# Staged tiles stored from ScalarE's queue, pair 0's splits three products earlier, down-stage loads in order of use

## The chip, the cores and the metric

The kernel runs on one core of one Trainium2 chip. The metric is the device time of one execution in microseconds (us); the time before is the median of three executions. TensorE multiplies; VectorE (DVE), ScalarE (ACT) and GpSimd (POOL) do the elementwise work; SyncE (SP) issues nearly all transfers between the chip's memory and SBUF. Every engine works through its own queue of instructions in order, and an instruction that has to wait holds what stands behind it in the same queue.

## What is computed

The reference is one layer of a flow model: a branch of state-space scans and a Fourier branch, gated and added to the residual, and then a gated feed-forward network with a final norm. The change lies in the feed-forward network:

```python
h2 = rmsnorm(x, p["norm2_g"]) * (1.0 + scale2) + shift2
ff = (jax.nn.silu(h2 @ p["w_ffn_gate"]) * (h2 @ p["w_ffn_up"])) @ p["w_ffn_down"]
x = x + gate2 * ff
```

There are 1152 tokens (1024 of the sample, 128 of the prompt), the model's width is 1024 and the hidden width 2816. All of it is in fp32.

## The kernel before, in words

**Up stage.** The hidden width is 22 tiles of 128, taken as 11 pairs, p = 0 to 10. For each pair `ffn_unit` (L1129 and on) runs a gate unit ("g") and an up unit ("u"). A unit multiplies a 2 x 2 arrangement of weight blocks by seven products, a Winograd scheme (Z W X Y Z X Y in the names of the PSUM banks), for two groups of tokens A and B. Each fp32 matmul is three matmuls in the fast fp32r form, on a high and a low part. So every weight operand is split: a cast on ScalarE (L962), then a subtraction on GpSimd or VectorE (L963). Sums of weight blocks (L1194 to L1210) are made on GpSimd. The unit's results are gated on ScalarE and GpSimd (L1188, L1190), stored to `ffd` in memory (L1229), and the sample's part of the pair is fetched again as `ra` (L1127) into the single buffer "gb".

**Operands for the down stage.** The down product is a Winograd scheme too, for pairs 0 to 8; pairs 9 and 10 use four ordinary products (STD). `a_steps(m)` makes pair m's seven operands out of `ra`, spread as hooks over the 14 products of the next pair's two units: for each a cast by ScalarE into a ring of three staging slots `stg` (L1307), the low part on VectorE (L1308), and a store to `ad` in memory (L1310). Pair 0 comes last, during pair 10's units. Three of its seven operands (ki 2, 3, 4) are not stored but stay in the staging ring. The list of hooks says after which product each step is issued; the first six products of the 14 have none:

```python
return [no, no, no, no, no, no, do(0), do(1), do(5), p6, do(p7a, 6), do(2), do(3), do(p7b, 4)]
```

**Down stage.** Block 0 is pair 0 alone; blocks 1 to 4 hold two pairs each (1 and 2, up to 7 and 8); then comes the STD block. `load_w` (L1394) fetches down weights `wd`, `prep` makes their Winograd sums (L1409) and splits them into `B` (L1362 and L1363; for pair 0 into `B0P`, with the subtraction on GpSimd), `load_at` (L1374) fetches operands `A` back from `ad`, `load_p` (L1405) the prompt's part `pr`, `load_a` (L1380) the raw tiles `fr` of pairs 9 and 10, and `x1_load` (L1535) the residual. The matmuls are on L1443, their sums into `acc` on L1460 and L1462. Pair 0's first two operands come as one tile `A1` in the buffer "gb", so their load waits for the last use of `ra0`.

**What sets the order.** The program is written as above, and a scheduler merges the pieces into one queue per engine by its own estimate of times. All loads and stores named here are in the SP queue. `tc.issue_after(x)` keeps an instruction behind x in the order. Tiles with the same tag share a ring of buffers, so a load waits until the last reader of the buffer's previous tile is done.

Of the kernel before, what the change touches and what calls it, by code (L numbers as in the profile page):

```python
# [19 lines left out]
NS = 1024  # L20
# [41 lines left out]
def tile_flow_step(ctx: ExitStack, tc: tile.TileContext, a, o):  # L62
    nc = tc.nc
    V, S, PL, PE, SY = nc.vector, nc.scalar, nc.gpsimd, nc.tensor, nc.sync
# [23 lines left out]
    def f32(ap):  # L88
        return ap.bitcast(F32)
# [38 lines left out]
    mods, last = {}, {}  # L128
# [179 lines left out]
    def load_w(q):  # L308
        wu[q] = weight(a["w_in"][q], f"us{q}", pool=pwu if q > 1 else None, eng=V)
# [24 lines left out]

    ada1_head()
    load_w(0)
    norm_stats(0)
    norm_tr(0)
    load_s5()
    load_w(1)  # L340
    h_scale0(range(4))
    u_first(0)
# [3 lines left out]
    norm_tr(1)  # L346
    run(ada1[5:])
    load_w(2)
    load_w(3)
    h_scale0(range(4, 8))  # L350
# [597 lines left out]
    x1d = dram.tile([9, 128, D], F32, tag="x1d", name="x1d")  # L948
# [150 lines left out]
    ffd = dram.tile([NF, 128, TOK], F32, tag="ffd", name="ffd")  # L1099
# [20 lines left out]
    LO, HI = slice(0, 512), slice(512, 1024)  # L1120
# [149 lines left out]
    hk, no = h2_hooks(2), (lambda: None)  # L1270
# [17 lines left out]
    ad = {m: dram.tile([7, 128, 2, 512], F32, tag=f"ad{m}", name=f"ad{m}") for m in range(STD[0])}  # L1288
# [3 lines left out]
    def a_steps(m):  # L1292
        a_ = {f"{f}{z}": ra[m][:, f, h] for f in range(2) for z, h in (("L", LO), ("H", HI))}

        def comb(out, x, y, op=ALU.subtract):
            V.tensor_tensor(a_[out], a_[x], a_[y], op)  # L1296

        def p6():
            comb("0H", "0H", "1H", ALU.add)
            comb("0L", "0H", "0L")  # L1300

        def one(ki):
            nonlocal nstg
            src = a_[dict(P1="0L", P2="1L", P6="0L", P7="0L", P4="1H", P5="0H", P3="1L")[KEYS[ki]]]
            st_ = stg[:, nstg % 3]
            nstg += 1
            S.copy(out=st_[:, 0], in_=src)  # L1307
            V.tensor_tensor(st_[:, 1], src, f32(st_[:, 0]), ALU.subtract)  # L1308
            if m or ki not in (2, 3, 4):
                SY.dma_start(out=ad[m][ki], in_=f32(st_))  # L1310

        def do(*fs):
            return lambda: [one(f) if isinstance(f, int) else f() for f in fs]

        p7a, p7b = (lambda: comb("1L", "1L", "0L")), (lambda: comb("0L", "1H", "0L"))
        return [no, no, no, no, no, no, do(0), do(1), do(5), p6, do(p7a, 6), do(2), do(3), do(p7b, 4)]

    for p in range(1, NF // 2):
        hk = a_steps((p - 1) % STD[0]) if p > 1 else [no] * 14
        ffn_unit(p, "g", "AB", hk[:7])  # L1320
        ffn_unit(p, "u", "AB", hk[7:])
        if p == 2:
            ffn_unit(0, "g", "B")
            ffn_unit(0, "u", "B")
            ra_load(2)
        if p == NF // 2 - 2:
            ra_load(0)
# [14 lines left out]
    AT, BT, PT, raws, araw, wraw = {}, {}, {}, {}, {}, {}  # L1342
# [9 lines left out]
    def wtile(name):  # L1352
        return ringed("w", [128, D], F32, "ws", NWS, "ws2", NW2, name)

    def a_new(name):
        return pA.tile([128, 2, 512], F32R, tag="A", bufs=NA, name=name)
# [9 lines left out]
    def load_at(m, ki):  # L1366
        key = KEYS[ki]
        if (m, key) in AT:
            return
        if m == 0 and ki in kept:  # L1370
            AT[m, key] = kept[ki]
            return
        AT[m, key] = A1[:, ki] if m == 0 and ki < 2 else a_new(f"A{m}_{ki}")
        SY.dma_start(out=f32(AT[m, key]), in_=ad[m][ki])  # L1374

    def load_a(m):
        araw[m] = []
        for f in range(2):
            t_ = pA.tile([128, NS], F32, tag="fr", bufs=NFR, name=f"fr{2 * m + f}")
            SY.dma_start(out=t_, in_=ffd[2 * m + f][:, 0:NS])  # L1380
            araw[m].append(t_)

    def load_w(m):
        if m in wraw:
            return
        wraw[m] = []
        for f in range(2):
            if m == 0 or (m == 1 and f == 0):
                w = wr.tile([128, D], F32, tag="ws", bufs=NWS, name=f"wd{2 * m + f}")
            elif m == 1:  # L1390
                w = wr.tile([128, D], F32, tag="fsA", name="wd3")
            else:
                w = wtile(f"wd{2 * m + f}")
            SY.dma_start(out=w, in_=a["w_d"][2 * m + f])  # L1394
            wraw[m].append(w)

    def load_raw(m):
        load_w(m)
        if m in STD:
            load_a(m)  # L1400
        raws[m] = [x[:, h] for x in wraw[m] + araw.get(m, []) for h in (LO, HI)]
# [9 lines left out]
    def prep(m, ki):  # L1411
        key = KEYS[ki]
        w0L, w0H, w1L, w1H = raws[m]
        if key == "P6":
            sub(w0H, w1H, w0H, eng=V if m in VSUB else PL)
            sub(w0L, w0H, w0L, ALU.add, V if m in VSUB else PL)
        if key == "P5":
            sub(w1L, w1L, w0L)
            sub(w0L, w1H, w0L)
        bsrc = dict(P1=w0L, P2=w1L, P6=w0L, P7=w0H, P4=w1L, P5=w0L, P3=w1H)[key]  # L1420
        if m == 0:
            B = wr.tile([128, 2, 512], F32R, tag="wh" if ki < 6 else "ftA", bufs=NWH if ki < 6 else 1, name=f"B0{key}")
        else:
            B = b_new(f"B{m}{key}")
        load_at(m, ki)
        BT[m, key] = split2(B, bsrc, PL if m == 0 else V)
# [97 lines left out]
    def x1_load(t, h=None):  # L1524
        nonlocal nx
        nx += 1
        if nx % 4 < 3:
            x = pA.tile([128, D], F32, tag="fr", bufs=NFR, name=f"x1_{t}{h}")
        else:
            x = pE.tile([128, D], F32, tag="xr", bufs=NXR, name=f"x1_{t}{h}")  # L1530
        if h is None:
            SY.dma_start(out=x, in_=x1d[t])
            return x
        x = x.rearrange("p (t c) -> p t c", t=2)
        SY.dma_start(out=x, in_=x1d[t:t + 2][:, :, HI if h else LO].rearrange("t p c -> p t c"))  # L1535
        return x

    def gate_x(i, j, r, eng=None):
        c = cc(i, j, r)
        x = x1_load(4 * i + 2 * r, j)  # L1540
        V.tensor_tensor(c, c, gH if j else gL, ALU.mult)  # L1541
        (eng or PL).tensor_tensor(c, c, x, ALU.add)
# [31 lines left out]
    def std_block():  # L1574
# [23 lines left out]
        for j in range(2):  # L1598
            prods(Q[:, j], [(PT[m][:, :, k], BT[m, (k, j)]) for m in STD for k in range(2)], True)
            add_to(accp[:, HI if j else LO], Q[:, j])  # L1600
        normal(1, 1, 1)
        x8 = x1_load(8)
        for j, h in enumerate((LO, HI)):
            V.tensor_tensor(accp[:, h], accp[:, h], g5p[:, h], ALU.mult)
# [52 lines left out]
    for ki in range(2):  # L1657
        for m in BLK[1]:
            load_at(m, ki)
# [124 lines left out]
```

## Time and profile before

| what | value |
|---|---|
| median of 3 executions | 1561.39 us (1560.08 to 1563.1) |
| the profiled execution | 1564.09 us, its span 1562.3 us |
| mean granted TensorE clock | 0.972 |
| TensorE busy | 1473.0 us, 94% of the span |
| VectorE / ScalarE / GpSimd busy | 937.5 / 563.9 / 662.9 us |
| DMA traffic | 243.84 MB, mean 156 GB/s |

A row of a timeline gives the start of an instruction (or of a run of equal ones, x12), its duration, the engine, the line, what it writes and reads with the sizes, and in brackets how long the engine had stood before it and what ended that. `ad<-stg` reads: written `ad`, read `stg`. A row of the waits gives the waiting engine and line, the engine that released it, the total, the number of times and the longest. SPq is the SP queue, and its durations are those of issuing, not of the transfer.

### The profile page before, as it was taken

How to read it: one execution, taken by the hardware profiler on the slowest of the kernel's cores; microseconds unless marked ns; L12 is line 12 of the kernel's file. 1: busy time of each engine (PE TensorE's matmuls, PEld its weight loads, DVE VectorE, ACT ScalarE, POOL GpSimd, SP SyncE). 2: the span in 40 equal slices, each digit the busy share in tenths (PEclk: the TensorE clock that was granted, in tenths of full speed). 3: DMA queues.
4: the chain of work that ended last, by engine and by line, in shares of the span. 5: the costliest groups of instructions: out<-in, count | busy, mean ns of one | idle time of the engine just before them, and what ended most of it. 6: DMA issues, size and time to landing. Idle time of an engine off the chain costs nothing. (4 is left out here: it accounts for less than half of the span.)

```text
span 1562.3 us, 24032 instructions
## 1 busy us (share of the span) xinstructions
PE 1473.0 (94%) x8999; PEld 1318.6 (84%) x8999; DVE 937.5 (60%) x1838; ACT 563.9 (36%) x1096; POOL 662.9 (42%) x606
## 2 busy tenths in 40 slices
PE   6999999999999999988999799999999979999995
PEld 3899998899977788866699799999999966888774
DVE  5648999994354345389923444454443445767778
ACT  7423334333643122345533243333333333211323
POOL 4900000000132112454697487787778872322354
PEclk9999999999989999999999899999999989999998
DMA  8242333222626634453523424544444549655423
GB/s 326 97 139 82 97 98 107 82 98 95 190 69 209 207 113 134 162 185 140 175 86 128 162 102 173 206 152 175 179 163 158 203 181 378 225 215 221 143 66 122
DMA packets 101985, 243.84 MB, mean 156 GB/s; under 512 B 15710, under 2 KB 46047, under 8 KB 101868
## 3 DMA queue, kind: packets, MB, share of 16 engines
q1 hardware_dynamic: 101868, 242.30, 44.1%
q8 instruction: 71, 1.16, 0.3%
q14 instruction: 46, 0.38, 0.1%
HBM read 172.51 MB, written 69.74 MB: 155 GB/s over the span
## 5 line engine op out<-in xcount | busy, mean ns | idle before, releaser
L94 POOL TENSOR_TENSOR wh_glu<-ws_glu,wh_glu 128x512 fp32r<-128x512 f32 x4 | 5.5, 1392 | 339.3 <-ACT wh_glu L93 339.3
L271 PE MATMUL g<-h,wh_g 128*128 128x384 f32 (+1 forms) x432 | 147.6, 342 | 0.0
L272 PE MATMUL g<-h,wh_g 128*128 128x384 f32 (+1 forms) x432 | 147.3, 341 | 0.0
L273 PE MATMUL g<-h,wh_g 128*128 128x384 f32 (+1 forms) x432 | 146.5, 339 | 0.0
L1308 DVE TENSOR_TENSOR stg<-ra,stg 128x512 fp32r<-128x512 f32 x63 | 79.9, 1279 | 88.3 <-ACT stg L1307 88.0
L1409 POOL TENSOR_TENSOR wd<-wd,wd 128x512 f32<-128x512 f32 x25 | 37.0, 1493 | 107.1 <-DMA wd<-in_w_d 52.9
L271 PEld LDWEIGHTS g<-h,wh_g 128*128 128x128 f32 x432 | 81.5, 189 | 0.3 <-issue 0.3
L272 PEld LDWEIGHTS g<-h,wh_g 128*128 128x128 f32 x432 | 81.6, 189 | 0.2 <-issue 0.2
L273 PEld LDWEIGHTS g<-h,wh_g 128*128 128x128 f32 x432 | 81.4, 188 | 0.2 <-issue 0.2
L94 POOL TENSOR_TENSOR wh_pj<-ws_pj,wh_pj 128x512 fp32r<-128x512 f32 x16 | 22.1, 1382 | 103.7 <-ACT wh_pj L93 94.2
L1462 DVE TENSOR_TENSOR acc<-acc,U 128x1024 f32<-128x1024 f32 x34 | 41.4, 1219 | 33.2 <-PE U L1443 32.8
L1307 ACT CAST stg<-ra 128x512 fp32r<-128x512 f32 x63 | 37.8, 616 | 61.2 <-DVE ra L1296 27.6
L963 DVE TENSOR_TENSOR wh_out<-ws_out,wh_out 128x512 fp32r<-128x512 f32 x32 | 33.8, 1071 | 24.6 <-ACT wh_out L962 24.6
L1443 PE MATMUL q<-B,A 128*128 128x512 f32 x192 | 45.7, 393 | 0.6 <-DVE acc L1462 0.4
L1443 PEld LDWEIGHTS q<-B,A 128*128 128x128 f32 x192 | 35.8, 187 | 9.6 <-DVE acc L1462 0.8
L963 POOL TENSOR_TENSOR wh_out<-ws_out,wh_out 128x512 fp32r<-128x512 f32 x16 | 21.9, 1373 | 50.6 <-ACT wh_out L962 47.6
L923 DVE TENSOR_TENSOR sgc<-sgc,p 128x384 f32<-128x384 f32 x24 | 13.3, 554 | 48.4 <-PE p L106 48.4
L977 PE MATMUL o<-wh_out,m 128*128 128x512 f32 x96 | 36.6, 409 | 4.5 <-ACT scr0b L1059 4.5
L636 DVE TENSOR_TENSOR ta<-X,Sg 128x56 f32<-128x56 f32 (+10 forms) x88 | 39.4, 448 | 1.1
L1190 POOL TENSOR_TENSOR fsA<-fsA,ftA 128x320 f32<-128x320 f32 x33 | 34.2, 1037 | 13.6 <-DVE ftA L1172 13.6
L639 DVE TENSOR_TENSOR X<-X,tb 128x56 f32<-128x56 f32 (+10 forms) x88 | 39.4, 456 | 0.9
L962 ACT CAST wh_out<-ws_out 128x512 fp32r<-128x512 f32 x48 | 28.3, 615 | 30.2 <-PE o L979 20.3
(1550 smaller groups left out, 4528.2 us busy)
## 6 DMA issues: line engine op xcount, KB each, us to landing
ad<-stg SPq DMA_DIRECT2D x60, 512.0 KB, 2.6
A<-ad SPq DMA_DIRECT2D x60, 512.0 KB, 6.1
wa<-in_w_ada SPq DMA_DIRECT2D x48, 512.0 KB, 5.7
ws_out<-in_w_out SPq DMA_DIRECT2D x24, 512.0 KB, 3.9
wd<-in_w_d SPq DMA_DIRECT2D x22, 512.0 KB, 6.4
ind<-in SPq DMA_DIRECT2D x54, 192.0 KB, 1.9
ws_g<-in_w_in SPq DMA_DIRECT2D x18, 512.0 KB, 3.5
sgc<-ind SPq DMA_DIRECT2D x48, 192.0 KB, 3.6
```

Of the source, the lines that this page charges most:

```text
L271: PE.matmul(ps, w[:, 0, wsl], hi, start=first, stop=False)
L272: PE.matmul(ps, w[:, 0, wsl], lo, start=False, stop=False)
L273: PE.matmul(ps, w[:, 1, wsl], hi, start=False, stop=last)
L636: V.tensor_tensor(A, src, Sc[:, 0, lv, gs].unsqueeze(1).unsqueeze(3).to_broadcast(shp), ALU.mult)
L639: V.tensor_tensor(dst, dst, B[:, ::-1], ALU.add)
L963: (eng or PL).tensor_tensor(w[:, 1, :], src, f32(w[:, 0, :]), ALU.subtract)
L977: PE.matmul(p, mc[t][0][:, k, ts_], w[n][:, 0], start=(k == 0), stop=False)
L1307: S.copy(out=st_[:, 0], in_=src)
L1308: V.tensor_tensor(st_[:, 1], src, f32(st_[:, 0]), ALU.subtract)
L1409: (eng or PL).tensor_tensor(out, x, y, op)
L1443: PE.matmul(ps, A[:, va], B[:, vb], start=(first and ti == 0 and i == 0), stop=(last and ti == n - 1 and i == 2), skip_group_check=True)
L1462: V.tensor_tensor(dst, dst, ps, ALU.add)
```

## The change

The stores of the staged operands are issued from ScalarE's queue (`S`) in place of SP's (`SY`). For pair 0 the eight steps start after three products without a hook in place of six, so three products earlier; its three empty places come at the end. The loads of `fr` and of the residual are held behind the last load of an operand `A` in the order, and the down weights of pairs 3 and up behind pair 1's second weight tile.

```diff
             if m or ki not in (2, 3, 4):
-                SY.dma_start(out=ad[m][ki], in_=f32(st_))
+                S.dma_start(out=ad[m][ki], in_=f32(st_))
...
-        return [no, no, no, no, no, no, do(0), do(1), do(5), p6, do(p7a, 6), do(2), do(3), do(p7b, 4)]
+        st = [do(0), do(1), do(5), p6, do(p7a, 6), do(2), do(3), do(p7b, 4)]
+        return [no] * 6 + st if m else [no] * 3 + st + [no] * 3
...
         AT[m, key] = A1[:, ki] if m == 0 and ki < 2 else a_new(f"A{m}_{ki}")
-        SY.dma_start(out=f32(AT[m, key]), in_=ad[m][ki])
+        last["A"] = SY.dma_start(out=f32(AT[m, key]), in_=ad[m][ki]).ins
...
-            SY.dma_start(out=t_, in_=ffd[2 * m + f][:, 0:NS])
+            with tc.issue_after(last["A"]):
+                SY.dma_start(out=t_, in_=ffd[2 * m + f][:, 0:NS])
...
-            SY.dma_start(out=w, in_=a["w_d"][2 * m + f])
+            with tc.issue_after(last["w3"]) if m > 2 else ExitStack():
+                i_ = SY.dma_start(out=w, in_=a["w_d"][2 * m + f]).ins
+            if m == 1 and f:
+                last["w3"] = i_
...
-            SY.dma_start(out=x, in_=x1d[t])
+            with tc.issue_after(last["A"]):
+                SY.dma_start(out=x, in_=x1d[t])
...
-        SY.dma_start(out=x, in_=x1d[t:t + 2][:, :, HI if h else LO].rearrange("t p c -> p t c"))
+        with tc.issue_after(last["A"]):
+            SY.dma_start(out=x, in_=x1d[t:t + 2][:, :, HI if h else LO].rearrange("t p c -> p t c"))
```

How the order moves is shown at three places. In these rows L1374, L1394, L1405 and L1662 of before are L1375, L1397, L1410 and L1669 of the change, and L1362 is L1363. The first place is the SP queue at the end of the up stage, before (`ws_u10AB` is the second weight tile of pair 10's up unit, `ad_7683` pair 0's stored operands, `A_12751` the tile of the first two):

```order
L1127 DMA ra_12259<-ffd 128x1024
L1229 DMA ffd<-fsA 128x2x640
L1127 DMA ra_12259<-ffd 128x1024
L1229 DMA ffd<-fstB 128x2x512
L957 DMA ws_u10AB_12493<-in_w_u 128x1024
L1394 DMA wd_12752<-in_w_d 128x1024
L1310 DMA ad_7683<-stg 128x1024
L1394 DMA wd_12754<-in_w_d 128x1024
L1310 DMA ad_7683<-stg 128x1024 x2
L1394 DMA wd_12787<-in_w_d 128x1024
L1310 DMA ad_7683<-stg 128x1024
L1374 DMA A_12751<-ad_7683 128x1024 x2
```

And the same place in the change:

```order
L1127 DMA ra_12259<-ffd 128x1024 x2
L1229 DMA ffd<-fsA 128x2x640
L1229 DMA ffd<-fstB 128x2x512
L957 DMA ws_u10AB_12501<-in_w_u 128x1024
L1397 DMA wd_12752<-in_w_d 128x1024
L1397 DMA wd_12754<-in_w_d 128x1024
L1397 DMA wd_12787<-in_w_d 128x1024
L1375 DMA A_12751<-ad_7683 128x1024 x2
```

The four stores are gone from this queue, and both halves of `ra0` (`ra_12259`) are fetched ahead of pair 9's stores. Further on, the `fr` and residual loads stand behind the last operand load; in the late unit of pair 0, the first weight load stands ahead of the store of `fsA`.

The second place is ScalarE at the boundary, before: from the cast of the third operand of pair 0 to the last (`ra_12259` is `ra0`; `B0P` are pair 0's weight operands).

```order
L1307 CAST stg<-ra_12259 128x512
L962 CAST wh_u10ABs_12702<-ws_u10AB_12491 128x512
L1362 CAST B0P_12756<-wd_12752 128x512
L1307 CAST stg<-ra_12259 128x512 x2
L1362 CAST B0P_12760<-wd_12754 128x512
L1307 CAST stg<-ra_12259 128x512
L1362 CAST B0P_12766<-wd_12752 128x512
L1362 CAST B0P_12771<-wd_12752 128x512
L1362 CAST B0P_12774<-wd_12752 128x512
L1307 CAST stg<-ra_12259 128x512
```

In the change, from the cast of the fourth operand to the last:

```order
L1307 CAST stg<-ra_12259 128x512
L1175 COPY ftA<-ZAu10AB 128x320
L1310 DMA ad_7683<-stg 128x1024
L1175 COPY fstB<-ZBu10AB 128x256
L1307 CAST stg<-ra_12259 128x512 x2
L962 CAST wh_u10ABs_12705<-ws_u10AB_12499 128x512
L1363 CAST B0P_12756<-wd_12752 128x512
L1363 CAST B0P_12760<-wd_12754 128x512
L1307 CAST stg<-ra_12259 128x512
L1363 CAST B0P_12766<-wd_12752 128x512
```

The last cast of `ra0` now stands ahead of the third `B0P` cast, and the stores are among ScalarE's own instructions, each behind VectorE's part of its operand.

The third place is GpSimd at the start of pair 10's gate unit, as a piece of the difference; pairs 4 to 9 change in the same way.

```order
 L963 TENSOR_TENSOR wh_u9ABs_12222<-ws_u9AB_12009,wh_u9ABs_12222 128x512
+L963 TENSOR_TENSOR wh_g10ABa_12275<-ws_g10AB_12262,wh_g10ABa_12275 128x512
 L1194 TENSOR_TENSOR s_g10AB<-ws_g10AB_12264 128x512
-L963 TENSOR_TENSOR wh_g10ABa_12275<-ws_g10AB_12262,wh_g10ABa_12275 128x512
 L1195 TENSOR_TENSOR ws_g10AB_12264<-ws_g10AB_12264,ws_g10AB_12262 128x512
 L1196 TENSOR_TENSOR ws_g10AB_12262<-s_g10AB,ws_g10AB_12262 128x512
 L1190 TENSOR_TENSOR fsA<-fsA,ftA 128x5x64
+L1190 TENSOR_TENSOR fstB<-fstB 128x4x64
 L963 TENSOR_TENSOR wh_g10ABs_12307<-ws_g10AB_12262,wh_g10ABs_12307 128x512
-L1190 TENSOR_TENSOR fstB<-fstB 128x4x64
```

The split of the unit's first operand, which reads the first weight tile, moves ahead of L1194, which reads the second; and group B's gating moves ahead of the split of the second operand.

## Rows read from the trace of the kernel before

**Rows 1.** The page's first part: busy us, share of the span, instructions.
```profile
PE 1473.0 (94%) x8999; PEld 1318.6 (84%) x8999; DVE 937.5 (60%) x1838; ACT 563.9 (36%) x1096; POOL 662.9 (42%) x606
```

**Rows 2.** TensorE's waits, whole span: what it waited for, us in total, times, longest.
```profile
PE U L1443 <- DMA A<-ad: 10.2, 1, 10.2
PE ZBg0B L1162 <- ACT wh_g0Ba L962: 7.6, 1, 7.6
...
PE WAu7AB L1162 <- POOL wh_u7ABs L963: 0.8, 1, 0.8
...
PE WAu8AB L1162 <- ACT wh_u8ABs L962: 0.7, 1, 0.7
```

**Rows 3.** Timeline of TensorE at the boundary: start us, us, instruction, idle before.
```profile
1268.92 1.56 PE L1162 MATMUL YBu10AB<-TB,wh_u10ABs 128*128 128x256 f32 x12
1280.68 4.62 PE L1443 MATMUL U<-B0P,A 128*128 128x512 f32 x12 [10.21 <-DMA A<-ad]
...
1287.94 2.96 PE L1443 MATMUL U<-B0P,stg 128*128 128x512 f32 x12
```

**Rows 4.** Timeline of VectorE at the boundary.
```profile
1276.37 0.82 DVE L1308 TENSOR_TENSOR stg<-ra,stg 128x512 fp32r<-128x512 f32 x1 [2.45 <-ACT stg L1307]
```

**Rows 5.** Timeline of the SP queue at the boundary.
```profile
1235.20 0.46 SPq L1127 DMA_DIRECT2D ra<-ffd  x1
...
1257.63 0.33 SPq L1394 DMA_DIRECT2D wd<-in_w_d  x1
1258.05 0.86 SPq L1310 DMA_DIRECT2D ad<-stg  x2
...
1268.22 0.32 SPq L1310 DMA_DIRECT2D ad<-stg  x1
1277.22 3.71 SPq L1374 DMA_DIRECT2D A<-ad  x8
```

**Rows 6.** Timeline of ScalarE at the boundary.
```profile
1264.61 1.14 ACT L1307 CAST stg<-ra 128x512 fp32r<-128x512 f32 x2 [6.84 <-DMA ad<-stg]
...
1274.68 1.14 ACT L1362 CAST B0P<-wd 128x512 fp32r<-128x512 f32 x2 [7.37 <-POOL wd L1409]
```

**Rows 7.** Windows: stretch, its us, busy us by engine, TensorE's clock, DMA share, GB/s.
```profile
1302.00:1323.00 21.00, 17.21 (x63) 12.39 (x62) 9.95 (x13) 5.92 (x10) 5.88 (x4) 0.92 1.04 400
...
1041.24:1225.57 184.33, 181.02 (x1347) 179.29 (x1345) 82.03 (x129) 62.53 (x131) 141.66 (x111) 0.99 0.46 172
```

**Rows 8.** Timeline of TensorE, first product of pairs 4 and 6.
```profile
952.48 0.32 PE L1162 MATMUL ZAg4AB<-TA,wh_g4ABa 128*128 128x320 f32 x1
...
1041.24 0.46 PE L1162 MATMUL ZAg6AB<-TA,wh_g6ABa 128*128 128x320 f32 x2
```

**Rows 9.** Timeline of GpSimd, start of pair 10's gate unit, and the boundary.
```profile
1218.48 1.28 POOL L1194 TENSOR_TENSOR s_g10AB<-ws_g10AB 128x512 f32<-128x512 f32 x1 [2.87 <-DMA ws_g10AB<-in_w_g]
1219.72 1.30 POOL L963 TENSOR_TENSOR wh_g10ABa<-ws_g10AB,wh_g10ABa 128x512 fp32r<-128x512 f32 x1
...
1262.09 1.30 POOL L1409 TENSOR_TENSOR wd<-wd,wd 128x512 f32<-128x512 f32 x1 [2.77 <-DMA wd<-in_w_d]
```

**Rows 10.** Timeline of the SP queue ahead of the late unit of pair 0.
```profile
873.65 0.32 SPq L1310 DMA_DIRECT2D ad<-stg  x1
...
874.80 0.51 SPq L1138 DMA_DIRECT2D ws_g0B<-in_w_g  x1
```

**Rows 11.** Instructions on the tile ad: count, ns min/median/max, first and last start; landing.
```profile
L1374 SPq DMA_DIRECT2D A<-ad x60: 319/320/814, 1277.2 to 1467.4; - x60
...
DMA to landing us min/median/max: 2.6/4.7/10.4
```

**Rows 12.** Timeline of ScalarE, first cast of fr.
```profile
1472.27 0.62 ACT L1362 CAST A<-fr 128x512 fp32r<-128x512 f32 x1 [4.24 <-PE X L1443]
```

**Rows 13.** Timeline of VectorE in pair 10's gate unit.
```profile
1221.86 3.16 DVE L1308 TENSOR_TENSOR stg<-ra,stg 128x512 fp32r<-128x512 f32 x2
```

**Rows 14.** Waits of the SP queue, whole span.
```profile
SPq L1310 <- DVE stg L1308: 167.0, 41, 14.9
```

## Prediction

> **What bounds the kernel now.** I read the page first, then TensorE's waits, then the timelines around the longest of them. TensorE is busy for nearly the whole span [rows 1], so a change can gain only where TensorE stands, or where it runs slower than it can. Three of its waits lie in the code that is touched [rows 2]: one of 10.2 us for the first Winograd operands of the down stage, one of 7.6 us in the late unit of pair 0, and, in the loop of units, waits under 1 us for GpSimd's or ScalarE's part of a weight split. What these add up to needs a window.
>
> The longest is the boundary between the stages. TensorE starts its last product at 1268.92, which takes 1.56 us, and then stands for 10.21 us; its first down-stage product then takes 4.62 us, where the same twelve matmuls take 2.96 us three products later [rows 3]. It waits for the load of two operands, issued at 1277.22. That load goes into the buffer of `ra0`, so it waits for the last L1308 on pair 0, which ends at 1277.19 and had itself waited 2.45 us for ScalarE's cast [rows 4]. The SP queue shows why the casts are late [rows 5]: the second half of `ra0` is fetched only at 1235.20, and two stores stand behind the weight load of 1257.63 and leave at 1258.05. ScalarE then stands 6.84 us for a landed store (the staging ring has three slots), and 7.37 us more behind casts of `B0P` that wait for GpSimd [rows 6]. The last cast comes behind those.
>
> After the boundary, in block 1, TensorE is busy 17.21 of 21 us while the DMA engines are busy throughout (a share of 1.04); over the four pairs from ZAg6 to ZAg10 it is busy 181.02 of 184.33 us [rows 7]. Four pairs in 184.33 us are 46.08 us a pair; from ZAg4 to ZAg6 two pairs took (1041.24 - 952.48) = 88.76 us, 44.38 a pair [rows 8]. So the later pairs lose 4 x 1.70 = 6.8 us. About half is standing (3.3 us), the rest slower running. GpSimd shows a cause [rows 9]: it stands 2.87 us for a weight tile ahead of L1194 and only then does the 1.30 us of L963 for `wh_g10ABa`, whose weights had arrived already.
>
> **The change, part by part.** The sum is made against the profiled execution, 1564.09 us, 2.7 us above the median of the runs, 1561.39.
>
> *Boundary: -11 us.* Three products earlier is 3/14 of a pair, 9.5 us by the 44.38. By the chain: both halves of `ra0` are fetched together near 1230, since no store stands ahead of them on SP. The stores leave from ScalarE as soon as VectorE's part is done, so no weight load is ahead of them. The last cast is now behind the casts for P1 and P2 alone, which read raw weights. The second of those tiles still cannot be fetched before its ring buffer is free, about 1257.63 [rows 5], and arrives when GpSimd's wait for it ends, 1262.09 [rows 9]. Two casts of 0.6 us and VectorE's 0.82 us, with 2 us for what is queued ahead, free the buffer near 1266. The first product began 3.46 us after the issue of the load [rows 3, 5]; so it could start near 1269.5, and TensorE is only done at 1268.92 + 1.56 = 1270.5. The wait goes (10.2), and with it the slow first product (4.62 - 2.96 = 1.7). I take 1 off, as the cover is just 1 us and the later `B0P` operands come out of GpSimd barely ahead of need. Ends: -12, and -2 if the cover breaks. What is late next is `B0P` for P6.
>
> *Block 1: -2 us.* Prompt operands and pair 1's second weight tile go ahead of four `fr` loads and weights used later. 3.8 us of standing are there to win [rows 7]. Ends -4 (all of it and some slow running) and +1.5, since the loads of operands and weights still share the same engines.
>
> *Loop of units: -5 us.* The store is taken off SP in every pair, and the order of GpSimd's work changes in every gate unit: L963 for the first product now fills the wait ahead of L1194. That takes 1.30 us a pair out of GpSimd's chain, against 1.70 lost [rows 8, 9]; over the four pairs 5.2 of 6.8. I take 5. Ends: -7 (all), +2 (ScalarE, which now stands for VectorE at each store, hands the loss back).
>
> *Late unit of pair 0: -1 us.* Its first weight load, at 874.80, goes ahead of a store, and the staging store at 873.65 leaves SP's queue [rows 10]; the 1.15 us between them is the price of the two. Ends -2.5 and 0 (the buffer may be free no earlier).
>
> *Tail: +0.5 us.* `fr` and `x1` loads now follow the last operand load, which before was issued at 1467.4 and a landing of which takes 2.6 to 10.4 us, 4.7 in the median [rows 11]. The first cast of `fr` came at 1472.27, released by TensorE [rows 12]; the load has 4.8 us for it, the third tile about as long. Ends -0.5 and +4 (each of four tiles late).
>
> *At nothing:* 60 stores cost ScalarE an issue each. SP's issue takes 0.32 us [rows 5], no trace here shows ScalarE's; at SP's price it is 19 us, spread over nine pairs and under waits that ScalarE has anyway. If that cover went, it would be rival D.
>
> **Sum:** -11 - 2 - 5 - 1 + 0.5 = -18.5. The profiled execution becomes about 1545.6, the median about 1543.
>
> The trace's rows price the queue at what stands ahead in it, up to several us a store. The Trainium skill, "DMA: Bandwidth & Descriptors", section "Issuing engines are not separate DMA queues", speaks against that: transfers from any engine run on the same 16 DMA engines, and a second issuer saves only the sequencer's time. By that rule alone the stores would give about 0.3 us each where they are on the path, and the boundary would be rival C. The trace has SP's sequencer standing, which the rule leaves to gain.
>
> **Rivals.** *B, the loop is not shortened:* ScalarE's standing for VectorE eats what GpSimd wins. For it: VectorE's two parts in a row took 3.16 us [rows 13], and a store now makes ScalarE wait for such. Against: the swap on GpSimd is plain in the order, and ScalarE's stores there stand behind other casts. It gives -11 - 2 + 0 - 1 + 0.5 = -13.5, so 1548.
>
> *C, the boundary stays:* the buffer is freed late whatever queue the stores use, by the weight tile of 1257.63 or by GpSimd's `B0P` chain, whose 7.37 us wait is in [rows 6]. Then the boundary gives -2 and the sum is -9.5: 1552. Against: the last cast now stands ahead of the `B0P` casts that wait for GpSimd.
>
> *D, slower:* ScalarE stands at its own stores. SP waited for VectorE's part ahead of 41 such stores, 167.0 us in all [rows 14], 4.1 us each; SP could afford it, while behind ScalarE's store stand the casts for TensorE's next products. The place is the W and Y operands of each gate unit from pair 3 on, eight units. If the 3.16 us of [rows 13] came on the path in each, the cost is 25 us, against -13.5 of the other parts: +11.5, so 1573. It decides from about 1.7 us a unit on (13.5 / 8), once the operands' lead is gone. Against: the longest wait of the loop for ScalarE is 0.7 us now [rows 2], so a lead is usually there. The same page of the Trainium skill, section "Anatomy of one DMA — SWDGE (gpsimd) path", says that a wait for a semaphore is made on the issuing sequencer, before dispatch. The trace agrees for SP with the 167.0 us; no run here shows it for ScalarE.
>
> *E, nothing moves:* what each part gains is taken again by another wait; 1561.
>
> **How the numbers follow.** Forecast 0.58; B 0.20; C 0.12; D 0.06; E 0.04. The changed code is plain to follow at the boundary, hence the large share of cases with that gain; the loop is the weakest term, hence B. Forecast alone spans about 1537 to 1548 (boundary -12, block 1 -4, loop -7 with the rest as taken at one end; loop -1 and tail +1.5 at the other). B and C reach to 1552.5. So the range is 1536.5 to 1552.5, leaving D, E and a little at either edge outside. Faster by over 0.2% (3.1 us, about what a measurement of this kernel can tell from no change): forecast, B and C, 0.90. Within it: E, 0.04. Slower: D, 0.06.
>
> **What would show it.** The boundary is right if the wait of TensorE's first U for `A` falls below 2 us and that product takes under 3.5 us; if it still waits over 5 us, C holds. Block 1 is right if the busy time in the 21 us after U for pair 1 starts is 19 or more. The loop is right if four pairs from ZAg6 to ZAg10 take under 180 us, and L1194 on GpSimd follows L963 with no wait over 2 us; at 184 us B holds. ScalarE waits for VectorE of some 3 us right ahead of weight casts, with TensorE waiting for L962, would be D. TensorE waiting for `A` from `fr` near the end would make the tail wrong. A time above 1552.5 would say that I missed a wait that the new order makes.

## The result and the profile after

The changed kernel takes 1547.4 us (median of 4, 1541.16 to 1549.33) against 1562.24 for the kernel before in the same runs (4, 1560.08 to 1563.1): a ratio of 0.990, interval 0.987 to 0.993. The forecast was 1543, range 1536.5 to 1552.5. A second series gave 1545.25 (ratio 0.989, 0.986 to 0.992). The profiled execution took 1545.5 us, with a span of 1543.5.

On the page TensorE is now busy 95% of a shorter span (94% in [rows 1]):

```profile
PE 1466.8 (95%) x8999; PEld 1316.9 (85%) x8999; DVE 938.4 (61%) x1838; ACT 567.0 (37%) x1096; POOL 663.4 (43%) x606
```

TensorE's waits, whole span (us in total, times, longest), answer to [rows 2]. The wait for `A<-ad` is gone from the list; a wait for ScalarE's copy `acc` and a longer wait of V near the end have come, and the late unit of pair 0 waits 5.5 us in place of 7.6, but then 3.7 for its next operand:

```profile
PE ZBg0B L1162 <- ACT wh_g0Ba L962: 5.5, 1, 5.5
...
PE WBg0B L1162 <- ACT wh_g0Bs L962: 3.7, 1, 3.7
PE U L1448 <- ACT acc L1465: 3.7, 1, 3.7
...
PE V L1448 <- DVE acc L1467: 2.5, 1, 2.5
...
PE WAu9AB L1162 <- POOL wh_u9ABs L963: 0.8, 1, 0.8
```

TensorE's timeline at the boundary answers to [rows 3]. The first down-stage product follows the last up-stage product at once and takes 2.97 us in place of 4.62. Three products on stands the new wait, and the product behind it is the slow one:

```profile
1262.14 1.56 PE L1162 MATMUL YBu10AB<-TB,wh_u10ABs 128*128 128x256 f32 x12
1263.54 2.97 PE L1448 MATMUL U<-B0P,A 128*128 128x512 f32 x12
...
1272.96 4.61 PE L1448 MATMUL U<-B0P,stg 128*128 128x512 f32 x12 [3.65 <-ACT acc L1465]
1277.41 2.96 PE L1448 MATMUL V<-B0P,stg 128*128 128x512 f32 x12
```

The windows (as in [rows 7]; the number ahead of the DMA share is TensorE's clock) show the loop of pairs 6 to 9, the 5 us after the new wait, and the start of block 1:

```profile
1039.61:1219.13 179.52, 178.04 (x1346) 177.52 (x1345) 81.28 (x128) 64.26 (x130) 141.96 (x111) 1.00 0.47 176
1273.00:1278.00 5.00, 5.00 (x15) 3.97 (x16) 2.35 (x2) 2.23 (x3) 1.50 (x2) 0.66 1.02 326
1288.93:1310.00 21.07, 21.07 (x93) 17.01 (x92) 17.38 (x20) 8.88 (x16) 7.74 (x5) 1.00 0.60 216
```

The four pairs take 179.52 us (184.33 before). After a stand of 3.65 us the granted clock was 0.66 on average for 5 us. Block 1, busy 17.21 of 21 us before, is busy all of its first 21.07 us.

To compare whole kernels I use five segments, each from the first product of one tile to the first of another in TensorE's timeline: **late** (ZAg2 to ZAg3, with the late unit of pair 0), **loop** (ZAg6 to ZAg10), **change of stage** (ZAg10 to the first U with B1P: the last pair and block 0), **blocks 1, 2** (first U with B1P to the first product with B5P) and **tail** (first product of the STD block to TensorE's end). The expectations below split the middle at another point: their "boundary" is ZAg10 to the first down-stage product, their "blocks 0 and 1" that product to the first with B5P; these values stand in the text where they decide.

| kernel | late | loop | change of stage | blocks 1, 2 | tail | time, us (ratio) |
|---|---|---|---|---|---|---|
| before | 78.69 | 184.33 | 76.70 | 89.71 | 63.85 | 1562.24 |
| changed | 78.20 | 179.52 | 69.80 | 83.13 | 65.40 | 1547.40 (0.990) |
| e1 stores only | 78.17 | 180.87 | 74.38 | 89.70 | 63.88 | 1553.87 (0.995) |
| e2 early steps only | 78.56 | 181.36 | 71.89 | 88.95 | 63.41 | 1556.15 (0.996) |
| e3 load order only | 78.50 | 185.25 | 76.60 | 84.37 | 63.08 | 1560.33 (0.999) |
| e4 GpSimd's order only | 78.69 | 179.67 | 74.63 | 89.73 | 61.89 | 1555.62 (0.996) |
| e5 stores, GpSimd's old order | 78.20 | 182.99 | 76.67 | 88.79 | 64.07 | 1561.86 (0.9995) |
| e6 all, but stores on SP | 78.81 | 179.93 | 70.67 | 83.11 | 62.76 | 1547.18 (0.990) |
| e7 copies on VectorE | 78.04 | 181.13 | 64.54 | 83.20 | 66.11 | 1541.76 (0.986) |
| e8 changed, again | 78.19 | 177.51 | 69.58 | 83.10 | 63.95 | 1545.25 (0.989) |
| e9 weights free | 77.98 | 180.32 | 71.24 | 85.03 | 65.00 | 1548.69 (0.993) |
| e10 residual early | 77.83 | 177.79 | 70.83 | 84.85 | 61.87 | 1541.82 (0.988) |
| e11 copies on VectorE, fr earlier | 78.12 | 180.30 | 64.31 | 83.19 | 63.29 | 1537.93 (0.985) |

Each segment comes from one profiled execution; each ratio is against the kernel before in the same runs. The ratios leave out two executions that were far longer than the rest, one of the kernel before (2412.55 us) and one of e3 (5877.35). The changed kernel's whole times spread by some 8 us, and code that no kernel here touches spreads as much: the feed-forward network's first product starts between 730.65 us (e6) and 739.95 (e7). So the segments say more on a part than the totals.

Of the 18.8 us between the two profiled spans, the segments hold -0.5 late, -4.8 loop, -6.9 change of stage, -6.6 blocks 1 and 2, and +1.6 tail, together -17.2. The rest, -1.6, lies ahead of ZAg2 and behind TensorE's end, in code that the change does not touch. The stretches between the segments (ZAg3 to ZAg6, and B5P to the STD block) differ by 0.05 us or less.

### The profile page after: what moved, and what is told of

Read it like the earlier page. It is cut to its first block, busy times and chain, and to the rows that moved or that the text cites. A ratio compares the mean times of both kernels' runs of the same rounds, so it can differ in the third digit from the quotient of the medians.

```text
span 1543.5 us, 23975 instructions
## 1 busy us (share of the span) xinstructions
PE 1466.8 (95%) x8999; PEld 1316.9 (85%) x8999; DVE 938.4 (61%) x1838; ACT 567.0 (37%) x1096; POOL 663.4 (43%) x606
## 5 line engine op out<-in xcount | busy, mean ns | idle before, releaser
L1308 DVE TENSOR_TENSOR stg<-ra,stg 128x512 fp32r<-128x512 f32 x63 | 69.4, 1112 | 72.2 <-ACT stg L1307 72.0
L963 DVE TENSOR_TENSOR wh_out<-ws_out,wh_out 128x512 fp32r<-128x512 f32 x32 | 33.8, 1071 | 24.6 <-ACT wh_out L962 24.6
L1296 DVE TENSOR_TENSOR ra<-ra 128x512 f32<-128x512 f32 x36 | 43.5, 1209 | 0.3
L963 POOL TENSOR_TENSOR wh_out<-ws_out,wh_out 128x512 fp32r<-128x512 f32 x16 | 22.4, 1405 | 48.8 <-ACT wh_out L962 45.7
```

The costliest lines, as they stand in the source:

```text
L963: (eng or PL).tensor_tensor(w[:, 1, :], src, f32(w[:, 0, :]), ALU.subtract)
```

## The experiments

**One part at a time: e1 to e3.** e1 has the new line for the store and nothing else:

```diff
-                SY.dma_start(out=ad[m][ki], in_=f32(st_))
+                S.dma_start(out=ad[m][ki], in_=f32(st_))
```

> The stores of the staged operands go from ScalarE's queue; pair 0's steps and the load order stay as before. Measures: loop = first product of pair 6 to first product of pair 10 (before 184.3 us, changed kernel 179.5); boundary = first product of pair 10 to first down-stage product (55.1 and 44.4); blocks 0 and 1 = first down-stage product to the first with B5P, block 3's (111.3 and 108.5). Theory (each part has its own place; the loop's gain comes with the stores, since only they change GpSimd's order): loop 179 to 181. Boundary: pair 0's steps are 9.5 us later than in the changed kernel, so TensorE still waits 5 to 8 us for A, boundary 49 to 52. Total about 1551. Rival (the stores alone make the boundary): boundary 44 to 46, wait for A under 2 us, total about 1546.

Measured: loop 180.87, and at the boundary a wait of 8.2 us (5 to 8 was expected), 52.8 us from pair 10's first product to the first down-stage product. TensorE's waits of e1 from 900 us on:

```profile
PE U L1443 <- DMA A<-ad: 8.2, 1, 8.2
```

So the stores shorten the loop, and alone they do not make the boundary. Nor are the 2 us that the wait lost mainly the queue's doing: of the runs below, e4 has its stores on SP and GpSimd's new order and waits 8.3 us, e5 has its stores on ScalarE and the old order and waits 9.3.

e2 has the new list of hooks and nothing else:

```diff
-        return [no, no, no, no, no, no, do(0), do(1), do(5), p6, do(p7a, 6), do(2), do(3), do(p7b, 4)]
+        st = [do(0), do(1), do(5), p6, do(p7a, 6), do(2), do(3), do(p7b, 4)]
+        return [no] * 6 + st if m else [no] * 3 + st + [no] * 3
```

> Only pair 0's steps are three products earlier; the stores stay in SP's queue. Theory: loop unchanged, 183 to 186 us. At the boundary one store still stands behind the weight load that waits for its ring buffer, so the ring of three slots holds the last casts up: TensorE waits 2 to 6 us for A, boundary 47 to 51, total about 1555. Rival (earlier steps do all of it): boundary 44 to 45, wait under 1 us. Rival (earlier steps do nothing while the stores are on SP): wait 8 us or more, total within 2 us of before.

Measured: a wait for `A` of 0.8 us and 45.6 us to the first down-stage product, close to the changed kernel's 44.4. This is the rival by which the earlier steps do all of it. TensorE's waits of e2 from 900 us on:

```profile
PE U L1444 <- ACT acc L1461: 5.4, 2, 4.7
...
PE U L1444 <- DMA A<-ad: 0.8, 1, 0.8
```

The SP queue of e2 shows why I had it wrong:

```profile
1258.67 0.33 SPq L1395 DMA_DIRECT2D wd<-in_w_d  x1
1259.22 0.32 SPq L1310 DMA_DIRECT2D ad<-stg  x1
...
1266.41 6.93 SPq L1375 DMA_DIRECT2D A<-ad  x8
```

A store does still stand behind the weight load, as I had said. But it is only one, and ScalarE's timeline of e2 shows what it cost the last cast:

```profile
1264.50 0.62 ACT L1307 CAST stg<-ra 128x512 fp32r<-128x512 f32 x1 [0.64 <-DMA ad<-stg]
```

0.64 us of standing. The operands' load leaves at 1266.41, in time. The wait that took the place of the old one, for ScalarE's `acc`, is here as well (4.7 us at its longest); so it comes with the earlier boundary, not with the stores. The loop took 181.36 us where 183 to 186 was expected, with GpSimd's order of before. So a single loop can differ by some 3 us with the order unchanged (184.33 before), and no single loop decides on it.

e3 has the rules on the loads and nothing else (of the diff, all parts behind the list of hooks).

> Only the load order is changed. Theory (block 1's gain comes from the order of loads): the wait for A at the boundary stays near 10 us, TensorE's waits in the 21 us around block 1's start fall from 3.8 to under 1.5 us, blocks 0 and 1 take 107 to 109 us in place of 111.3, and the tail (first product of the standard block to the end) takes 65 to 66 in place of 63.9; total about 1560. Rival (block 1 gained because the boundary came earlier and the transfers had time): blocks 0 and 1 stay at 110 to 112.

Measured: a wait of 10.2 us at the boundary, as before; blocks 0 and 1 take 106.0 us in place of 111.3 (107 to 109 was expected), blocks 1 and 2 84.37 in place of 89.71. In time e3 cannot be told from before (0.9991, 0.9976 to 1.0005): the interval reaches to -3.7 us, so the 5.3 us of the segment, from one profiled execution, are not all seen in the time, and no run shows where the rest goes. Its window of 21 us on block 1's start, which answers to [rows 7], first row:

```profile
1302.87:1324.00 21.13, 20.40 (x88) 15.99 (x87) 16.36 (x19) 8.98 (x16) 8.22 (x5) 1.00 0.69 254
```

TensorE is busy 20.40 of 21.13 us and at the full clock, where it had been busy 17.21 of 21 at 0.92. The order of loads does this by itself, without the earlier boundary. What TensorE stood for in that stretch before was the following, behind two waits of 0.68 and 0.67 us for ScalarE's copies:

```profile
1315.23 0.50 PE L1443 MATMUL Xp<-B2P,P 128*128 128x512 f32 x1 [1.19 <-DVE P L1363]
...
1316.52 0.50 PE L1443 MATMUL Xp<-B1P,P 128*128 128x512 f32 x1 [0.55 <-DVE acc L1462]
1317.72 0.73 PE L1443 MATMUL Y<-B1P,A 128*128 128x512 f32 x2 [0.71 <-DVE B1P L1363]
```

Half of the 3.8 us, 1.19 and 0.71, is thus waiting for VectorE's split of the prompt's part (`P`) and of `B1P`. In e3 neither is left, nor the wait for the addition; one of 0.68 us for ScalarE's copy is. The tail was 63.08, not the expected 65 to 66.

**What shortens the loop: e4 and e5.** The stores changed two things at once: the queue, and through the scheduler GpSimd's order. e4 forces the new order while the stores stay in SP's queue (the first pair of lines gives the split's subtraction a name):

```diff
-        (eng or PL).tensor_tensor(w[:, 1, :], src, f32(w[:, 0, :]), ALU.subtract)
+        last["lo"] = (eng or PL).tensor_tensor(w[:, 1, :], src, f32(w[:, 0, :]), ALU.subtract).ins
...
-        PL.tensor_tensor(s1, a21, a22, ALU.add)
+        with tc.issue_after(last["lo"]) if gate_ and p > 3 else ExitStack():
+            PL.tensor_tensor(s1, a21, a22, ALU.add)
```

> The kernel before, stores in SP's queue, with only GpSimd's order of the changed kernel forced in the gate units of pairs 4 to 10 (the split of the first operand ahead of L1194). Theory (the loop's gain is GpSimd's order): loop 179 to 181 us, everything else as before, total about 1557. Rival (the loop's gain is that SP's queue is free of stores, so that weight tiles are fetched sooner): loop 183 to 186, total as before.

e5 has the stores on ScalarE's queue, and L1194 forced ahead of the split in the same units:

```diff
+        with tc.issue_after(after) if after else ExitStack():
+            (eng or PL).tensor_tensor(w[:, 1, :], src, f32(w[:, 0, :]), ALU.subtract)
...
+        late_ = gate_ and p > 3
+        i_ = PL.tensor_tensor(s1, a21, a22, ALU.add).ins if late_ else None
+        h = split(a11, nm + "a11", le(0), after=i_)
...
```

> Stores from ScalarE's queue as in e1, but GpSimd's order of before forced in the gate units of pairs 4 to 10 (L1194 ahead of the split of the first operand). Theory (the loop's gain is GpSimd's order, and the queue of the stores gives nothing by itself): loop 182 to 186 us, total 1557 to 1562. Rival (the stores off SP's queue shorten the loop by themselves): loop 179 to 181, total about 1554 as in e1.

Measured: e4 has a loop of 179.67 and a ratio of 0.9958 (0.9944 to 0.9971); e5 has a loop of 182.99 and a ratio of 0.9995 (0.998 to 1.001). GpSimd's timeline at the start of pair 10's gate unit, in the changed kernel (answering to [rows 9]):

```profile
1209.56 1.73 POOL L963 TENSOR_TENSOR wh_g10ABa<-ws_g10AB,wh_g10ABa 128x512 fp32r<-128x512 f32 x1
1212.00 1.29 POOL L1194 TENSOR_TENSOR s_g10AB<-ws_g10AB 128x512 f32<-128x512 f32 x1 [0.70 <-DMA ws_g10AB<-in_w_g]
```

in e4 (L1195 there is L1194 of the others):

```profile
1208.67 1.74 POOL L963 TENSOR_TENSOR wh_g10ABa<-ws_g10AB,wh_g10ABa 128x512 fp32r<-128x512 f32 x1
1211.70 1.74 POOL L1195 TENSOR_TENSOR s_g10AB<-ws_g10AB 128x512 f32<-128x512 f32 x1 [1.29 <-DMA ws_g10AB<-in_w_g]
```

and in e5 (L1195 and L964 there are L1194 and L963):

```profile
1215.68 1.42 POOL L1195 TENSOR_TENSOR s_g10AB<-ws_g10AB 128x512 f32<-128x512 f32 x1 [2.33 <-DMA ws_g10AB<-in_w_g]
1217.06 1.30 POOL L964 TENSOR_TENSOR wh_g10ABa<-ws_g10AB,wh_g10ABa 128x512 fp32r<-128x512 f32 x1
```

With the split first, the wait for the weight tile is 0.70 or 1.29 us; with the old order 2.33 (2.87 before), and the split comes behind it. All nine loops with the new order lie between 177.5 and 181.1 us, mean 179.7; the four with the old one between 181.4 and 185.3, mean 183.5. The order is worth 3.8 us by these two means, and the queue by itself nothing that the time shows. The Trainium skill ("DMA: Bandwidth & Descriptors", "Issuing engines are not separate DMA queues") has it that a second issuer saves only the sequencer's time for issuing. These runs agree: 0.9995 for the queue alone.

The two groups of loops nearly touch (181.13 in e7, 181.36 in e2); what decides is that the whole times of e4 and e5 stand apart too. GpSimd's order had changed in a second way, group B's gating moving ahead of the split of the second operand. That move is in e4 and in e5 alike; here it is in e5 (L1191 there is L1190):

```profile
1223.01 0.74 POOL L1191 TENSOR_TENSOR fstB<-fstB 128x256 f32<-128x256 f32 x1
1223.71 3.50 POOL L964 TENSOR_TENSOR wh_g10ABs<-ws_g10AB,wh_g10ABs 128x512 fp32r<-128x512 f32 x2
```

So it is the split ahead of L1194 that counts. e4 was expected to leave all else as before; the wait for `A` at the boundary fell with it, from 10.2 to 8.3 us.

**Everything but the queue: e6.** The changed kernel with the store's line of before, and e4's edit for GpSimd.

> The changed kernel with the stores back in SP's queue, and GpSimd's order of the changed kernel forced. Theory (the change of queue matters only through the order that came with it): loop 179 to 181 us, boundary 45 to 47, blocks 0 and 1 108 to 111, total 1546 to 1550, within 2 us or so of the changed kernel. Rival (ScalarE's queue gives a gain of its own): 1553 or more, with TensorE waiting 3 us or more for A at the boundary.

Measured: 1547.18 us, 0.9904 (0.9869 to 0.9938), as the changed kernel. TensorE's waits of e6 from 900 us on:

```profile
PE U L1449 <- ACT acc L1466: 3.9, 1, 3.9
...
PE U L1449 <- DMA A<-ad: 0.3, 1, 0.3
```

0.3 us for `A`, and the same wait for ScalarE's copy. The late segment is the only one that goes with the queue: 77.8 to 78.2 us in the eight kernels with the stores on ScalarE, 78.5 to 78.8 in the five with them on SP, 0.6 us in the mean.

**The new wait: e7, with e8 beside it.** ScalarE's timeline of the changed kernel at the boundary:

```profile
1266.56 1.66 ACT L1363 CAST B0P<-wd 128x512 fp32r<-128x512 f32 x3 [6.02 <-POOL wd L1414]
1271.38 0.62 ACT L1363 CAST B0P<-wd 128x512 fp32r<-128x512 f32 x1 [3.16 <-POOL fsA L1190]
1271.90 1.92 ACT L1465 COPY acc<-U 128x1024 f32<-128x1024 f32 x2
```

The two copies of the first sums stand behind casts of `B0P`, which wait for GpSimd, the last of them until 1271.38 for the buffer of the up stage's last gating. Both sums had been complete since 1263.54 + 2.97 = 1266.5. VectorE, which adds the next sums, had nothing to do. e7 gives it the copies:

```diff
             prod(U[r], ms, "P1", r, True)
-            add_to(cc(0, 0, r), U[r], first)
+            if first:
+                V.tensor_copy(out=cc(0, 0, r), in_=U[r])
+            else:
+                add_to(cc(0, 0, r), U[r])
```

> The changed kernel, with the two copies of block 0's first sums (product P1) on VectorE in place of ScalarE. Theory (the 3.65 us wait that the second U of block 0 has in the changed kernel is ScalarE's copy standing behind casts of B0P that wait for GpSimd): the wait falls under 1 us, the product takes 2.96 us in place of 4.61, blocks 0 and 1 take 103 to 105 us in place of 108.5, total about 5 us below the changed kernel. Rival (GpSimd is late with B0P itself): the wait turns into one for B0P of over 2 us, and blocks 0 and 1 stay above 107.

e8 is the changed kernel once more.

> The changed kernel once more, to see how far its segments spread: loop 179 to 182 us, boundary 44 to 45, blocks 0 and 1 108 to 109, tail 62 to 66, total 1541 to 1549.

Measured: VectorE's copy and TensorE's second U in e7:

```profile
1272.28 1.23 DVE L1479 COPY acc<-U 128x1024 f32<-128x1024 f32 x1 [1.15 <-PE U L1448]
```

```profile
1276.28 2.96 PE L1448 MATMUL U<-B0P,stg 128*128 128x512 f32 x12
```

No wait stands before that U, and it takes 2.96 us. Blocks 0 and 1 take 103.2 us (103 to 105 was expected) against 108.3 in e8, and the change of stage 64.54 against 69.58; the operands `B0P` themselves are in time. The medians are 1541.76 and 1545.25, their intervals overlap. In e8 the loop, 177.51 us, came under the 179 to 182 that was expected; the other segments came as expected.

**Which rule on the loads counts: e9 and e10.** e9 lets the weights go free again, e10 the `fr` and residual loads (the second edit, at each of the three loads):

```diff
-            with tc.issue_after(last["w3"]) if m > 2 else ExitStack():
+            with ExitStack():
```

```diff
-            with tc.issue_after(last["A"]):
+            with ExitStack():
```

> The changed kernel without the rule that holds the down weights of pairs 3 and up behind pair 1's second tile. Block 1 and 2 segment = first product with B1P to first with B5P: 89.7 us before, 83.1 in the changed kernel. Theory (the four fr and four x1 loads, 4 MB among the first operand loads, made block 1 stand): the segment stays at 83 to 84.5. Rival (the weights' order made it): 86 to 90, with waits for P or B1P in block 1.

> The changed kernel with the fr and x1 loads free to go early again, the weights still held. Theory: the segment from the first product with B1P to the first with B5P goes back to 87 to 90 us with 2 to 4 us of waits in block 1, and the V product near the end waits 1.6 us or less in place of 2.2 to 2.5. Rival (the weights' order made it): 83 to 84.5.

Measured: 85.03 and 84.85 us for blocks 1 and 2, against 83.1 to 83.2 with both rules (84.4 in e3) and 88.8 to 89.7 with neither. Theory and rival fall, both of them: no one rule is the cause. Each alone does some 4.5 of the 6.3 us, and the second adds the rest. Their windows on the start of block 1, e9 and then e10:

```profile
1290.47:1312.00 21.53, 20.18 (x86) 15.67 (x85) 15.26 (x19) 8.35 (x15) 6.99 (x5) 1.00 0.46 167
```

```profile
1287.65:1309.00 21.35, 20.14 (x86) 15.69 (x85) 14.91 (x17) 8.36 (x15) 7.99 (x5) 1.00 0.97 371
```

e10 moves 371 GB/s there, with a DMA share of 0.97, and TensorE is busy 20.14 of 21.35 us; e9 moves 167 and TensorE is no better off. So the volume beside block 1 is not by itself what made it stand. TensorE's waits there are 0.68 and 0.68 us for ScalarE's copies in e9, and 0.68 for a copy and 0.54 for ScalarE's cast of `P` in e10; the two waits of before for VectorE's splits are gone in both. What is left is the place in the queue of what these splits read (the prompt's part and pair 1's second weight tile, which either rule moves forward). The waits fit it, but no run moves it alone. In e10 V waits 1.6 us near the end, as before, in place of 2.5.

**A further version: e11.** e7, and the `fr` loads put ahead of the last four operand loads:

```diff
-        last["A"] = SY.dma_start(out=f32(AT[m, key]), in_=ad[m][ki]).ins
+        last["A"] = last["A", m, ki] = SY.dma_start(out=f32(AT[m, key]), in_=ad[m][ki]).ins
...
-            with tc.issue_after(last["A"]):
+            with tc.issue_after(last["A", 8, 4]):
                 SY.dma_start(out=t_, in_=ffd[2 * m + f][:, 0:NS])
```

> The changed kernel with the copies on VectorE (as e7) and the fr loads ahead of the last four operand loads, which wait for ring buffers. Theory: blocks 0 and 1 stay at 103 to 104 us (first down-stage product to the first with B5P), ScalarE no longer waits for fr, the V product's wait near the end falls from 2.5 to 1.6 us, total 1538 to 1543. Rival (the tail's wait has nothing to do with fr): V still waits 2.2 us or more.

Measured: 1537.93 us (1534.98 to 1541.64), 0.9851 (0.9828 to 0.9874), the lowest median of all; its interval overlaps those of e7, e10 and both series of the changed kernel. TensorE's wait of V from 900 us on, and ScalarE's first cast of `fr`, released by TensorE as it was in [rows 12]:

```profile
PE V L1448 <- DVE acc L1467: 1.6, 1, 1.6
```

```profile
1449.03 0.62 ACT L1363 CAST A<-fr 128x512 fp32r<-128x512 f32 x1 [4.24 <-PE X L1448]
```

Against the changed kernel as profiled in e8 the segments differ by -5.3 at the change of stage and -0.7 in the tail.

## Why the prediction was right, step by step

**The sum** was -18.5 for the profiled execution and -17.2 was found in its segments (-18.8 with untouched code). That it came so close is in part luck: two terms were off by 4 us and more, in opposite directions. By the medians the gain was 14.8 us in the first series and 17.3 in the second, so the forecast gain was a little too large: the profiled execution of before lies 1.9 us above its median, that of the changed kernel 1.9 below.

**Boundary: -11 forecast, -6.9 found** in the change of stage. The first half held word for word: the wait of 10.2 us went, the first product takes 2.97 us, and the load of the operands left early enough. SP's timeline of the changed kernel shows it, answering to [rows 5]:

```profile
1257.39 8.69 SPq L1375 DMA_DIRECT2D A<-ad  x8
```

TensorE was done with the up stage 6 us later. The step that failed is "what is late next is `B0P` for P6". It was ScalarE's copy of the first sums, queued behind casts of `B0P`. I had checked when GpSimd has the operands ready, not what else stands in ScalarE's queue behind the casts that wait for them. It cost 3.65 us of standing and 1.65 of slow running (4.61 against 2.96), in sum 5.3. Rival C had the right place, GpSimd's `B0P` chain, and the wrong victim. The reason I gave for the gain was wrong as well in part: I put it on the stores' queue and the early steps together. e2 shows that the early steps do nearly all of it.

**Block 1: -2 forecast, -6.6 found** in blocks 1 and 2, outside my end of -4. The direction and the part of the change were right (e3 has it with nothing else changed), the size was not. Standing of 3.8 us was there to win, and I took half of it, fearing that the loads would still share the engines. All of it went, and with it the clock of 0.92 in that stretch, which I had given next to nothing. In e10 the engines are shared nearly as much as before (371 and 400 GB/s), and TensorE loses 1.2 us there in place of 3.8, no more than in e9 at 167.

**Loop: -5 forecast, -4.8 found,** in the mean of all kernels -3.8. The mechanism was the forecast one, GpSimd's split moved into the wait ahead of L1194. Rival B's gain of 0 is excluded: with the new order the seven loops with the stores on ScalarE take 179.6 us in the mean, the two with them on SP 179.8 (184.33 before), so ScalarE's standing ate nothing. What the prediction left together, the stores and the order, e4 and e5 take apart: it is the order.

**Late unit: -1 forecast, -0.5 found.** The first wait fell by 2.1 us (7.6 to 5.5) and the next rose by 1.3 (2.4 to 3.7). The second was this before:

```profile
PE WBg0B L1162 <- ACT wh_g0Bs L962: 2.4, 1, 2.4
```

The second half of the weights had gained less than the first: GpSimd's sum that reads it starts at 882.50 before and at 880.63 in the change, and 1.1 us of that is the earlier start of the whole stretch (ZAg2 at 829.35 and 828.26).

**Tail: +0.5 forecast, +1.6 found,** with a spread as large. One reading behind the forecast was wrong: I took a landing of 4.7 us from [rows 11], which is the median over the stores and the loads of `ad` together. The page gives them apart:

```profile
ad<-stg SPq DMA_DIRECT2D x60, 512.0 KB, 2.6
A<-ad SPq DMA_DIRECT2D x60, 512.0 KB, 6.1
```

A load's 6.1 us are more than the 4.8 that I had for it. In the changed kernel a landing of `fr` took 6.0 us, and the casts did wait. With the `fr` and residual loads held, the tail took 62.8 to 66.1 us (six runs, mean 64.4), without 61.9 to 64.1 (six, mean 63.2). What is certain is the wait: ScalarE's casts of `fr` in the changed kernel, where [rows 12] had TensorE as the releaser, now wait for the load:

```profile
1453.91 0.62 ACT L1363 CAST A<-fr 128x512 fp32r<-128x512 f32 x1 [0.94 <-DMA fr<-ffd]
...
1456.52 1.15 ACT L1363 CAST A<-fr 128x512 fp32r<-128x512 f32 x2 [0.77 <-DMA fr<-ffd]
...
1459.00 0.62 ACT L1363 CAST A<-fr 128x512 fp32r<-128x512 f32 x1 [0.82 <-DMA fr<-ffd]
```

and V waits 2.2 to 2.5 us in every kernel with both held, 1.6 in every other, as in the kernel before:

```profile
PE V L1443 <- DVE acc L1462: 1.6, 1, 1.6
```

**Rival D** did not come, though the standing it rests on did: in the changed kernel's loop none of the waits that the profile lists for TensorE is for ScalarE any more, but ScalarE stands at its stores, some 40 us in all by the gaps ahead of them in its timeline. The longest gaps come once in each of pairs 4 to 9, 1.7 us each, as here from 1201.65 on:

```profile
1201.05 0.60 ACT L1307 CAST stg<-ra 128x512 fp32r<-128x512 f32 x1
1203.34 0.33 ACTq L1310 DMA_DIRECT2D ad<-stg  x1
1203.74 0.47 ACT L1188 ACTIVATE fsA<-ftA 128x320 f32<-128x320 f32 x1 [2.08 <-DVE ftA L1172]
```

VectorE's part of that operand ended at 1203.30, and the store left then. That a wait is made on the issuing sequencer, as the Trainium skill has it ("DMA: Bandwidth & Descriptors", "Anatomy of one DMA — SWDGE (gpsimd) path"), agrees with these rows. 1.7 us a unit is where the prediction let the rival decide, once the operands' lead is gone; TensorE did not wait, so the lead held.

**The signs** that were named: the wait of U for `A` below 2 us and the product under 3.5 (none, 2.97), block 1 busy 19 of 21 us or more (21.07 of 21.07), the loop under 180 us (179.52) and no wait over 2 us ahead of L1194 in the gate unit (0.70), all came. The sign for the tail, TensorE waiting for `A` from `fr`, came in a milder form, by way of V.

## What to carry to other kernels

When a scheduler sets the order, an edit to one queue can do its work in another: here moving 60 stores to another queue gave 0.6 us in one segment and nothing that the whole time shows, and the order of two GpSimd instructions that came with it gave 3.8 us. Compare the orders of all engines, and try the order by itself. When a wait ahead of a stage goes, follow not only the operands of the next product but every instruction queued behind the ones that produce them; two copies in the wrong queue gave back almost half of the gain at the boundary (5.3 of some 12 us), and moved to an idle engine they gave no wait. For loads, look first at what stands ahead of the needed one: how busy the transfers were did not tell the loss here.

## What was not expected of the hardware

In the changed kernel a stand of 3.65 us was followed by as slow a product (4.61 us for twelve matmuls that take 2.96) as one of 10.21 us in the kernel before (4.62). Over all kernels, stands of 3.5 to 4.7 us were followed by products of 4.35 to 5.49 us (the changed kernel, e2, e6, e8, e9 and e10), stands of 8.2 to 10.2 us by 4.61 to 4.77 (before, e1, e3 and e4). So a short wait of TensorE cost 1.4 to 2.5 us more than its length, and a long one 1.65 to 1.8. The granted clock shows a difference in when: in the first microsecond of the slow product it was 0.76 behind the short stand and 0.50 (1.2 GHz) behind the long one, and in both it was 1.00 again (2.4 GHz) from 4 us after the start.

A share of the DMA engines of 0.97 over 21 us (e10) went with a TensorE that lost 1.2 us, one of 0.46 (e9) with 1.4, and one of 1.04 before the change with 3.8 us of standing: the share told little about the loss.
